# Split weights of the channel-major blocks: one fixed place in their tiles, or one of 16 places in turn

## The chip, the cores and the metric

The kernel runs on one core of a Trainium2 chip. The metric is the device time of one execution in microseconds (us), the median over several runs. The core has five engines with queues of their own: TensorE multiplies matrices, VectorE and ScalarE work element by element, GpSimd does small work and issues some transfers, and SyncE issues the weight transfers. On TensorE the loading of weights (the stationary operand) and the matmul that streams the other operand past them are recorded apart, as PEld and PE.

## The reference

One layer of a hybrid encoder for 256 tokens of width 2048, in float32. The normed input `n` is projected to queries, keys and values of a gated delta rule and of a dilated window attention; both are mixed by `w_out` and added to the residual stream. Then comes a gated MLP with a short convolution, and a last norm.

```
h = h + W_out [ GatedDeltaNet_bidir(n) ; DilatedWindowAttn(n) ],   n = RMSNorm(h)
up = conv3( RMSNorm(h) @ w_ffn_in )            # 2048 -> 2 x 5632
h = h + ( silu(gate) * val ) @ w_ffn_out       # 5632 -> 2048
out = RMSNorm(h)
```

The change touches the products with `w_in` (those for q, k, v and z of the delta rule and q and k of the attention) and with `w_ffn_in`.

## The kernel before

**Split products.** A float32 product is made of three matmuls on rounded parts: weights and activations are both split in a high part (the value as TensorE's fp32r type keeps it) and a low part (the rest). A product adds high x high, high x low and low x high. The activations lie split in `xcat`, for each of 16 tiles of 128 input channels 256 high and then 256 low columns, one for each token.

**Items.** A weight matrix comes in chunks of 1 MB over SyncE's queue into one of four tiles `raw`. A chunk is used in items of 1024 values for each partition. `split(u)` (line 257) has ScalarE copy an item's values into the high tile `his[u % 4]` (line 265) and VectorE subtract that from the raw values into the low tile `los[u % 4]` (line 266). The item's attribute `at` says at which float of these tiles, which are 1152 floats long, the 1024 values begin. `run_items` runs through all items in order: it keeps three items split ahead, issues an item's 24 matmuls (12 with 512 columns), and then gives other work (convolutions, attention, the delta rule's steps) a share of the engines' time; that work's own small matmuls and transposes come between the items on TensorE's queue.

**Channel-major blocks.** `cm_block` computes 128 output channels for all tokens. It has two items (input channels 0 to 1023 and 1024 to 2047), each with eight sets of 128 columns of weights. For each set the three lines 314, 315 and 316 load high, high and low weights, and stream the 256 high, 256 low and 256 high columns of `xcat`. All its items have `at = AT_CM = 32`. There are 80 such blocks in the input projection (24 for q, k and v of the delta rule, 8 for z, 48 for q and k of the attention) and 88 in the up projection, where all four tiles `his` and `los` are used in turn.

**Token-major items.** The values of the attention (`v_slab`, lines 382 to 384) take `xcat` as weights and stream the split weights in 256 columns, with `at = 0`. The output projection (`tm_group`, lines 1224 to 1226) loads the split mixed activations and streams split weights in 512 columns, with `at = AT_OUT = 72`; the last projection uses the same lines on `gth` and `gtl` with `at = 0`.

The order of the input projection is: 24 blocks, 8 blocks, then four times 12 blocks and three value slabs. In the up projection, the items of the first four blocks are interleaved, and after the transposes of the second norm (lines 1279 and 1298) no other work has matmuls until the end of that stage.

Of the kernel before, what the change touches and what calls it, by code (L numbers as in the profile page):

```python
# [24 lines left out]
NU = 4  # L25
LA = 3

AT_CM, AT_OUT = 32, 72
BV = 1300
BA = 1500  # L30
WAIT_FIRST = 8
# [54 lines left out]
def block_kernel(tc, A, out, dbg=None):  # L86
# [73 lines left out]
    done = set()  # L160
# [133 lines left out]
    def in_slab(w, c0, kh):  # L294
        return w[kh * 1024 : (kh + 1) * 1024, c0 : c0 + 256].rearrange("(k p) c -> p k c", p=P)

    accn = [0]

    def next_acc():
        accn[0] += 1  # L300
        return accs[accn[0] % len(accs)]

    def cm_block(ch, j, done, width=P):

        box = {}

        def half(kh):
            def mms(hi, lo):
                if kh == 0:
                    box["acc"] = next_acc()  # L310
                acc = box["acc"][:width, :T]
                for kk in range(8):
                    k = kh * 8 + kk
                    mm(acc, lhsT=hi[:, kk, :], rhs=xcat[:, k, :T], start=k == 0, stop=False)  # L314
                    mm(acc, lhsT=hi[:, kk, :], rhs=xcat[:, k, T:], start=False, stop=False)  # L315
                    mm(acc, lhsT=lo[:, kk, :], rhs=xcat[:, k, :T], start=False, stop=k == KT - 1)  # L316

            return mms

        for kh in range(2):  # L320
            Item(ch[kh], lambda t, j=j: t[:, :, j * width : (j + 1) * width], half(kh),
                 (lambda: done(box["acc"])) if kh else None, AT_CM)

    def evac(out_ap, acc, n=P, perm=None):

# [35 lines left out]
    def slab(w, c0, mk):  # L361
        ch = [Chunk(in_slab(w, c0, kh), (8, 256)) for kh in range(2)]
        for j in range(2):
            cm_block(ch, j, mk(j))
# [941 lines left out]
    for s in range(FT // 2):  # L1306
        if s == 0:
            ch = [Chunk(in_slab(w_up, w * FF, kh), (8, 256)) for kh in range(2) for w in range(2)]
            ch = [ch[0::2], ch[1::2]]
        else:  # L1310
            ch = [[Chunk(in_slab(w_up, w * FF + s * 256, kh), (8, 256)) for kh in range(2)] for w in range(2)]
        for w in range(2):
            for j in range(2):
                cm_block(ch[w], j, lambda acc, w=w, f=2 * s + j: hooks["up"](w, f, acc))
        if s == 0:
            items[-8:] = items[-8::2] + items[-7::2]
# [168 lines left out]
```

## Time and profile before

| | |
|---|---|
| median of 3 runs | 1546.69 us (1545.17 to 1550.15) |
| the profiled execution | 1545.1 us |
| its span, first to last instruction | 1543.3 us |
| TensorE busy | 1514.2 us, 11,531 matmuls |
| weight loads | 1443.4 us, 11,531 |
| VectorE busy | 1039.9 us |
| ScalarE busy | 827.9 us |
| GpSimd busy | 164.5 us |
| moved by the transfers | 301.20 MB, mean 195 GB/s |

A record of a matmul lasts longer than the distance to the next one's start, since matmuls overlap in the array. So a rate is read from starts in the timeline and from counts in a stretch, not from the length of a record. The stages in time are: input projection to about 700 us (the values of the attention in four portions from 292 us on), output projection to 797, up projection to 1295, last projection to 1536.

### The profile page before, as it was taken

What the parts mean: (1) busy time and instruction counts of PE and PEld (TensorE: products, weight loads), DVE (VectorE), ACT (ScalarE), POOL (GpSimd) and SP (SyncE); (2) the same over time, 40 slices, a digit from 0 to 9 for tenths busy, and PEclk for the clock granted to TensorE, in tenths of its full rate; (3) what the DMA queues carried; (4) which work ended last, traced back from release to release, by engine and by line L of the source; (5) the groups of instructions that cost most, each with busy time, mean ns of one, the idle gap of its engine ahead of it and who ended that gap; (6) DMA issues with size and microseconds to landing.
All of it is one profiled execution on the core that took longest, in us unless ns stands there. A gap on an engine that the chain in (4) does not pass through costs nothing.

```text
span 1543.3 us, 28173 instructions
## 1 busy us (share of the span) xinstructions
PE 1514.2 (98%) x11531; PEld 1443.4 (94%) x11531; DVE 1039.9 (67%) x1703; ACT 827.9 (54%) x1430; POOL 164.5 (11%) x245
## 2 busy tenths in 40 slices
PE   7999998999999999999999999999999999999997
PEld 7999998999999999997889999999999999888886
DVE  5878976979864666665557767677676676455454
ACT  5598874545555646554555544544544544344342
POOL 3264552000012202100000000000000000000000
PEclk9999999999999999999999999999999999999999
DMA  9656789646558636634765555565655657566552
GB/s 255 219 184 223 233 294 214 203 145 204 183 142 258 206 122 204 199 124 151 272 217 184 173 191 192 172 209 167 198 185 179 203 165 260 197 210 207 191 191 82
DMA packets 247283, 301.20 MB, mean 195 GB/s; under 512 B 10981, under 2 KB 207766, under 8 KB 246770
## 3 DMA queue, kind: packets, MB, share of 16 engines
q1 hardware_dynamic: 235602, 269.81, 54.4%
q0 software_dynamic: 11120, 29.01, 6.1%
q8 instruction: 90, 1.47, 0.4%
q10 hardware_dynamic: 432, 0.59, 0.1%
q14 instruction: 39, 0.32, 0.1%
HBM read 285.69 MB, written 13.65 MB: 194 GB/s over the span
## 4 chain that ended last, share of the span: by engine, by line
PE 91%; DMA 3%; ACT 2%; issue 2%; DVE 1%; POOL 1%; POOLq 0%; SPq 0%; ACTq 0%; DVEq 0%
PE bank L314 19%; PE bank L316 19%; PE bank L315 19%; PE bank L1224 7%; PE bank L1225 7%; PE bank L1226 7%; PE bank L382 3%; PE bank L383 3%; PE bank L384 3%; DMA raw<-in_w_in_dram 1%; PE bank L978 1%; PE bank L1024 1%; ACT hi L265 1%; PE bank L1019 1%; ACT kb L748 1%
## 5 line engine op out<-in xcount | busy, mean ns | idle before, releaser
L266 DVE TENSOR_TENSOR lo<-raw,hi 128x1024 fp32r<-128x1024 f32 x504 | 619.3, 1230 | 399.9 <-ACT hi L265 397.5
L265 ACT ACTIVATE hi<-raw 128x1024 fp32r<-128x1024 f32 x504 | 533.5, 1060 | 548.7 <-PE bank L315 262.5
L314 PE MATMUL bank<-xcat,hi 128*128 128x256 f32 x2688 | 758.4, 282 | 5.4 <-ACT qk L329 5.1
L315 PE MATMUL bank<-xcat,hi 128*128 128x256 f32 x2688 | 751.8, 280 | 0.0
L316 PE MATMUL bank<-xcat,lo 128*128 128x256 f32 x2688 | 751.6, 280 | 0.0
L314 PEld LDWEIGHTS bank<-xcat,hi 128*128 128x128 f32 x2688 | 506.2, 188 | 8.4 <-ACT qk L329 5.5
L315 PEld LDWEIGHTS bank<-xcat,hi 128*128 128x128 f32 x2688 | 512.0, 190 | 0.0
L316 PEld LDWEIGHTS bank<-xcat,lo 128*128 128x128 f32 x2688 | 505.6, 188 | 0.0
L1226 PE MATMUL bank<-hi,gtl 128*128 128x512 f32 x336 | 130.7, 389 | 0.0
L1225 PE MATMUL bank<-lo,gth 128*128 128x512 f32 x336 | 130.7, 389 | 0.0
L1224 PE MATMUL bank<-hi,gth 128*128 128x512 f32 x336 | 130.7, 389 | 0.0
L382 PE MATMUL bank<-hi,xcat 128*128 128x256 f32 x384 | 109.2, 284 | 0.0
L384 PE MATMUL bank<-hi,xcat 128*128 128x256 f32 x384 | 106.9, 278 | 0.0
L383 PE MATMUL bank<-lo,xcat 128*128 128x256 f32 x384 | 106.8, 278 | 0.0
L1224 PEld LDWEIGHTS bank<-hi,gth 128*128 128x128 f32 x336 | 63.1, 188 | 13.2
L1226 PEld LDWEIGHTS bank<-hi,gtl 128*128 128x128 f32 x336 | 63.1, 188 | 13.1
L1225 PEld LDWEIGHTS bank<-lo,gth 128*128 128x128 f32 x336 | 63.1, 188 | 13.0
L382 PEld LDWEIGHTS bank<-hi,xcat 128*128 128x128 f32 x384 | 72.4, 188 | 0.5
L384 PEld LDWEIGHTS bank<-hi,xcat 128*128 128x128 f32 x384 | 72.5, 189 | 0.0
L383 PEld LDWEIGHTS bank<-lo,xcat 128*128 128x128 f32 x384 | 72.3, 188 | 0.0
L1388 DVE SCALAR_TENSOR_TENSOR fy<-fpad,cwf,fy 128x256 f32<-128x256 f32 x132 | 63.4, 480 | 2.3
L1418 POOL DMA_DIRECT2D nfb<-in_norm_final_w_dram x1 | 0.6, 585 | 485.7 <-PE bank L316 485.7
(299 smaller groups left out, 1439.2 us busy)
## 6 DMA issues: line engine op xcount, KB each, us to landing
raw<-in_w_in_dram SPq DMA_DIRECT2D x104, 1024.0 KB, 5.7
raw<-in_w_ffn_in_dram SPq DMA_DIRECT2D x88, 1024.0 KB, 5.2
raw<-in_w_ffn_out_dram SPq DMA_DIRECT2D x44, 1024.0 KB, 5.0
raw<-in_w_out_dram SPq DMA_DIRECT2D x14, 1024.0 KB, 5.1
rec_d<-rec POOLq DMA_DIRECT2D x8, 768.0 KB, 7.1
rr<-rec_d POOLq DMA_DIRECT2D x6, 512.0 KB, 4.7
xt<-in_x_dram SPq DMA_DIRECT2D x4, 512.0 KB, 8.4
gam<-cg_d POOLq DMA_DIRECT2D x8, 256.0 KB, 8.7
```

The costliest lines, as they stand in the source:

```text
L265: ACT(hi, src, AF.Copy)
L266: V.tensor_sub(lo, src, hi.bitcast(F32))
L314: mm(acc, lhsT=hi[:, kk, :], rhs=xcat[:, k, :T], start=k == 0, stop=False)
L315: mm(acc, lhsT=hi[:, kk, :], rhs=xcat[:, k, T:], start=False, stop=False)
L316: mm(acc, lhsT=lo[:, kk, :], rhs=xcat[:, k, :T], start=False, stop=k == KT - 1)
L382: mm(o, lhsT=xh, rhs=hi[:, kk, :], start=k == 0 and t == 0, stop=False, skip_group_check=True)
L383: mm(o, lhsT=xh, rhs=lo[:, kk, :], start=False, stop=False, skip_group_check=True)
L384: mm(o, lhsT=xl, rhs=hi[:, kk, :], start=False, stop=k == KT - 1, skip_group_check=True)
L1224: mm(a[t], lhsT=xh, rhs=hi[:, kk, :], start=st, stop=False)
L1225: mm(a[t], lhsT=xh, rhs=lo[:, kk, :], start=False, stop=False)
L1226: mm(a[t], lhsT=xl, rhs=hi[:, kk, :], start=False, stop=sp_)
L1388: stt(y, pad[:, d : d + T], cwf[:, d, b : b + 1], y, op0=ALU.mult, op1=ALU.add)
```

## The change

`AT_CM` goes. `cm_block` counts its calls, and a block's two items begin at float `8 * (n % 16)` of their tiles, where n is the block's number, from 1 on: 8, 16, ... 120, 0, 8, and so on. A float has 4 bytes, so neighbouring blocks lie 32 bytes apart, modulo 512. The value slabs stay at 0, the output projection at 72, the last projection at 0.

```diff
-AT_CM, AT_OUT = 32, 72
+AT_OUT = 72
+AT_STEP, AT_N = 8, 16
...
-    accn = [0]
+    accn, blocks = [0], [0]
...
     def cm_block(ch, j, done, width=P):
 
         box = {}
+        blocks[0] += 1
+        at = AT_STEP * (blocks[0] % AT_N)
...
             Item(ch[kh], lambda t, j=j: t[:, :, j * width : (j + 1) * width], half(kh),
-                 (lambda: done(box["acc"])) if kh else None, AT_CM)
+                 (lambda: done(box["acc"])) if kh else None, at)
```

## Rows read from the trace of the kernel before

**Rows 1.** The page: busy time by engine; the chain that ended last, by line.
```profile
PE 1514.2 (98%) x11531; PEld 1443.4 (94%) x11531; DVE 1039.9 (67%) x1703; ACT 827.9 (54%) x1430; POOL 164.5 (11%) x245
...
PE bank L314 19%; PE bank L316 19%; PE bank L315 19%; PE bank L1224 7%; PE bank L1225 7%; PE bank L1226 7%; PE bank L382 3%; PE bank L383 3%; PE bank L384 3%; DMA raw<-in_w_in_dram 1%; PE bank L978 1%; PE bank L1024 1%; ACT hi L265 1%; PE bank L1019 1%; ACT kb L748 1%
```

**Rows 2.** Stretches: start:end, length, then PE, PEld, DVE, ACT, POOL; clock, DMA, GB/s.
```profile
25.00:293.00 268.00, 262.33 (x2270) 258.36 (x2269) 215.35 (x414) 193.35 (x443) 101.52 (x143) 0.99 0.76 230
293.00:700.00 407.00, 403.56 (x3433) 395.76 (x3432) 287.84 (x545) 226.10 (x435) 41.40 (x69) 1.00 0.57 179
...
812.00:1295.00 483.00, 483.00 (x4103) 483.00 (x4103) 342.20 (x514) 244.11 (x346) 0.00 (x0) 1.00 0.57 187
1295.00:1536.00 241.00, 239.75 (x1060) 198.22 (x1058) 119.32 (x116) 96.36 (x103) 4.37 (x6) 1.00 0.56 189
```

**Rows 3.** Timeline of TensorE's matmuls, input projection: start, length, line, operands.
```profile
370.13 0.28 PE L314 MATMUL bank<-xcat,hi 128*128 128x256 f32 x1
...
379.99 0.28 PE L314 MATMUL bank<-xcat,hi 128*128 128x256 f32 x1
```

**Rows 4.** Timeline of TensorE's matmuls, up projection.
```profile
1000.16 0.28 PE L314 MATMUL bank<-xcat,hi 128*128 128x256 f32 x1
...
1009.70 0.28 PE L314 MATMUL bank<-xcat,hi 128*128 128x256 f32 x1
```

**Rows 5.** Timeline of TensorE's matmuls, the last restart in the up projection.
```profile
811.39 0.60 PE L1298 MATMUL bank<-cst,ss 128*128 128x128 f32 x4
811.75 0.36 PE L314 MATMUL bank<-xcat,hi 128*128 128x256 f32 x1
...
812.19 0.28 PE L314 MATMUL bank<-xcat,hi 128*128 128x256 f32 x1
...
812.54 0.28 PE L314 MATMUL bank<-xcat,hi 128*128 128x256 f32 x1
```

**Rows 6.** Timeline of TensorE's matmuls, first and last item matmul of the input projection.
```profile
25.12 0.28 PE L314 MATMUL bank<-xcat,hi 128*128 128x256 f32 x1
...
698.04 0.28 PE L384 MATMUL bank<-hi,xcat 128*128 128x256 f32 x1
```

**Rows 7.** Timeline of TensorE's matmuls, passage from a channel-major block to values.
```profile
399.37 0.28 PE L314 MATMUL bank<-xcat,hi 128*128 128x256 f32 x1
...
399.71 0.28 PE L382 MATMUL bank<-hi,xcat 128*128 128x256 f32 x1
...
400.06 0.28 PE L382 MATMUL bank<-hi,xcat 128*128 128x256 f32 x1
...
400.41 0.28 PE L382 MATMUL bank<-hi,xcat 128*128 128x256 f32 x1
```

**Rows 8.** Timeline of TensorE's matmuls, an earlier passage of the same kind.
```profile
292.11 0.28 PE L314 MATMUL bank<-xcat,hi 128*128 128x256 f32 x1
...
292.46 0.29 PE L382 MATMUL bank<-hi,xcat 128*128 128x256 f32 x1
...
292.82 0.28 PE L382 MATMUL bank<-hi,xcat 128*128 128x256 f32 x1
...
293.16 0.28 PE L382 MATMUL bank<-hi,xcat 128*128 128x256 f32 x1
```

**Rows 9.** Groups by line and form on VectorE, 797 to 1295 and 1295 to 1524 us.
```profile
L266 DVE TENSOR_TENSOR lo<-raw,hi 128x1024 fp32r<-128x1024 f32 x176 | 215.7, 1225 | 142.4 <-ACT hi L265 141.5
...
L266 DVE TENSOR_TENSOR lo<-raw,hi 128x1024 fp32r<-128x1024 f32 x84 | 102.5, 1225 | 112.7 <-ACT hi L265 112.7
```

**Rows 10.** Timeline of TensorE's matmuls, output projection and last projection.
```profile
717.11 0.39 PE L1224 MATMUL bank<-hi,mxh 128*128 128x512 f32 x1
...
717.79 0.39 PE L1224 MATMUL bank<-hi,mxh 128*128 128x512 f32 x1
...
1399.95 0.39 PE L1224 MATMUL bank<-hi,gth 128*128 128x512 f32 x1
...
1400.63 0.39 PE L1224 MATMUL bank<-hi,gth 128*128 128x512 f32 x1
```

## The prediction, made before the changed kernel ran

> **What bounds the kernel now.** I read the page first. TensorE is busy for 98% of the span, and of the chain of work that ended last 19% each lies on lines 314, 315 and 316, the three matmuls of a channel-major product [rows 1]. The stretches by stage say the same more sharply: from 812 to 1295 us, the up projection, TensorE is busy for 483.00 of 483.00 us while VectorE works for 342 and ScalarE for 244, and the last projection, 1295 to 1536, is nearly as full [rows 2]. So nothing feeds TensorE too late there; the time is the number of matmuls times the step from one start to the next.
>
> That step has two values. Between 370.13 and 379.99 us lie 87 steps in 9.86 us, 113.33 ns each [rows 3]; between 1000.16 and 1009.70 lie 81 steps in 9.54 us, 117.78 ns each [rows 4]. Both stretches run the same lines on operands of one shape, from the same tiles, with the split weights at the same place in them (32), at a granted clock of 1.00, the 2.4 GHz level [rows 2]. I call them the short and the long step; the difference is 117.78 - 113.33 = 4.45 ns a matmul.
>
> Which one runs is decided at a restart and then stays. After the four small matmuls of line 1298, line 314 restarts at 811.75 us; its next start, at 812.19, contains the restart, and from there three steps take 0.35 us (3 x 117.8 = 353 ns; three short ones would take 340) [rows 5]. It stays long through 4,103 matmuls, the count of the stretch [rows 2], over all four tiles, eight weight positions in each, and four accumulators. From the first to the last channel-major or value matmul of the input projection (first and last row in [rows 6], 4,992 starts between and with them) I count the 4,991 steps between neighbours: 3,091 short, 1,656 long, and 244 others, which are restarts, the first few matmuls after one, and some 3 us of doubled steps near 270 us. Of 103 uninterrupted runs there, 63 settle on the short step and 40 on the long one, and none changes later of itself.
>
> One event changes it without an interruption: the passage between the channel-major products, whose weights lie at 32 in the split tiles, and the value products (lines 382 to 384), which stream the split tiles from 0 and take their weights from xcat. At 399.71 us the short step becomes long (three steps take 0.34 us before it, 0.35 and 0.35 after) [rows 7], at 292.46 long becomes short (0.35 before, 0.36 in the passage, 0.34 after) [rows 8], and at 329.68, 437.44 and 520.31 the same view shows short to long twice and long to short once. Five passages, five flips. At such a passage the placement changes, but so do the roles of the tiles.
>
> **The change part by part.** It removes and adds no instruction, no DMA and no wait, and moves nothing in any queue. It moves where the 168 channel-major blocks (80 of the input projection, 88 of the up projection) keep their split weights: block n starts at 8 x (n mod 16) floats instead of 32. Reads and writes of one item move together.
>
> Splitting itself: VectorE writes the low part of an item in 1225 ns with the weights at 32, and in 1225 ns in the last projection with them at 0 [rows 9]. I take nothing, and half of the last digit (0.5 ns) an item either way; TensorE's work hides it in the up projection, where VectorE is idle for 141 of 483 us [rows 2]. Without that cover, 336 items would give 0.2 us.
>
> The matmuls: the moved weights are the operand that TensorE loads. The output projection streams its split weights from 72, the last projection from 0, with 512 columns, and both step by 0.68 us for three, 226.7 ns [rows 10]. So 288 and 0 bytes do not differ for a streamed operand; a loaded one at another place is nowhere in the trace by itself. Its cost is bounded by the two steps: if every block boundary could set the step anew, the up projection gains at most 4,103 x 4.45 = 18.3 us (all short) and at least nothing (all long, as now); a longer step at this clock is in no row, and I take none. In the input projection only what lies behind a block boundary inside an uninterrupted run can change: 1,296 matmuls on the short step (+5.8 us if all turn long) and 240 on the long one (-1.1 us).
>
> I take the passages of [rows 7, 8] as the nearest rows: a jump in the placement between two matmuls that follow each other is what flips the step, and from now on there is one at every block boundary. If each boundary flips it, half of the up projection runs short: -9.1 us; in the input projection somewhat over half of the 1,296 turn long and of the 240 short, +3.3 - 0.6 = +2.7. Together -6.4. If instead a boundary acts as a restart, 63 of 103 come up short: -11.2 in the up projection, 0.39 x 5.8 - 0.61 x 1.1 = +1.6 before, together -9.6. The middle is -8.0 us. The output and last projections and the 48 value items keep their places; the values' restarts may fall otherwise, which I leave in the range.
>
> The profiled execution took 1545.1 us (span 1543.3 and 1.8 around it), 1.6 below the median of 1546.69. 1545.1 - 8.0 = 1537.1, and 1538.7 at the median's level. Its own range is 1533 to 1543.
>
> **The rivals.**
>
> *The place plays no part*: 1546.7. For it: the step stays at one value while loads go over four tiles and eight positions in each [rows 2, 4], both steps occur at place 32 [rows 3, 4], and 72 and 0 do not differ when streamed [rows 10]. The flips at the passages could come from the exchange of roles alone. Against it: those positions differ by whole 128-column blocks, and a shift inside one block appears only at the passages. The Trainium skill, SBUF — State Buffer, section "A bandwidth-pool intuition that's wrong (but worth ruling out)", gives TensorE's weight load a read port of its own beside the streaming operand's. By that rule where the loaded weights lie could not disturb the stream, and the sum would be 0; no row here tests it, and the two steps at one and the same place agree with it so far.
>
> *Short everywhere*: a boundary releases the long step and nothing brings it back. -18.3 - 1.1 = -19.4, 1527.3. For it: after a restart the short step is the commoner one, 63 of 103 [rows 6], and two passages led to it; against: three of five passages went from short to long.
>
> *Slower*: a boundary breaks the short step and leaves the long one. Its place is the input projection, whose uninterrupted short runs of more than a block hold the 1,296 matmuls; the up projection has nothing to lose, since it runs long already. +5.8, 1552.5; with all 3,091 short steps of the input projection made long it would be +13.8, 1560.4. It decides from the point where the long step outlasts the boundaries of the up projection. For it: the three passages from short to long, and 4,103 matmuls without a way out; against: two passages out of the long step.
>
> **How the numbers follow.** Forecast 0.40, no part 0.29, short everywhere 0.14, slower 0.17. Below 0.3% (4.6 us, about what can be told from no change here), so between 1542.1 and 1551.3, lie the second case, a small part of the forecast (0.05) and of the last (0.03). Faster 0.35 + 0.14 = 0.49; same 0.05 + 0.29 + 0.03 = 0.37; slower 0.14. The range from 1525 to 1554 holds all but the far end of the last case (1560.4) and an up projection all short whose input projection's restarts turn short as well.
>
> **What would show it.** In the changed kernel's view of TensorE from about 812 to 1290 us, steps of 0.113 and 0.118 must alternate in stretches of 48 matmuls or multiples, with the change at a first matmul of line 314 of a block; the up projection must then last about 474 us in place of 483. One step throughout with 483 us says that the place plays no part; 465 us that short wins; a longer input projection (25 to 700 us) with an unchanged up projection is the slower case. A step above 0.118 in some blocks, or VectorE's splits off 1225 ns, would make the prediction wrong in a way I have no row for.

## The result, and the profile after

The changed kernel took 1556.67 us (median of 4 runs, 1555.06 to 1556.94), the kernel before 1548.42 beside it (4 runs): a ratio of 1.0061, 95% interval [1.0046, 1.0076]. It is slower, by 0.6%. The forecast was 1538.7, and the range ended at 1554.

The page of the changed kernel, in the two rows that answer to [rows 1] (lines below 300 have moved down by 1, those from 314 on by 3):

```profile
PE 1529.1 (98%) x11531; PEld 1458.8 (94%) x11531; DVE 1041.2 (67%) x1703; ACT 828.4 (53%) x1430; POOL 162.4 (10%) x245
...
PE bank L317 19%; PE bank L319 19%; PE bank L318 19%; PE bank L1227 7%; PE bank L1228 7%; PE bank L1229 7%; PE bank L385 3%; PE bank L387 3%; PE bank L386 3%; DMA raw<-in_w_in_dram 1%; PE bank L981 1%; PE bank L1027 1%; PE bank L1022 1%; ACT kb L751 1%; DMA rec_d<-rec 1%
```

TensorE is still the bound, with the same number of matmuls, and takes longer for them. The stretches that answer to [rows 2], with the same columns, and one more, from 830 to 1270 us, which lies inside the up projection in every kernel below:

```profile
25.00:293.00 268.00, 263.27 (x2228) 259.56 (x2227) 211.71 (x409) 191.25 (x441) 99.49 (x143) 0.99 0.74 224
293.00:700.00 407.00, 407.00 (x3428) 399.74 (x3426) 286.31 (x529) 223.51 (x422) 40.64 (x67) 1.00 0.58 180
812.00:1295.00 483.00, 483.00 (x4084) 483.00 (x4083) 340.27 (x519) 242.06 (x343) 0.71 (x1) 1.00 0.57 185
1295.00:1536.00 241.00, 241.00 (x1111) 201.59 (x1111) 121.92 (x118) 101.22 (x110) 3.43 (x5) 1.00 0.58 197
...
830.00:1270.00 440.00, 440.00 (x3718) 440.00 (x3717) 310.76 (x469) 220.76 (x314) 0.00 (x0) 1.00 0.57 187
```

From 830 to 1270 us TensorE is busy throughout at a granted clock of 1.00, so the length by the count is the step: 440 / 3718 = 118.34 ns. The same stretch of the kernel before reads:

```profile
830.00:1270.00 440.00, 440.00 (x3739) 440.00 (x3738) 311.57 (x469) 219.95 (x314) 0.00 (x0) 1.00 0.57 187
```

That is 117.68 ns. This one row measures the step of the up projection in every kernel below.

The timeline shows what the steps depend on. In the changed kernel, TensorE's first channel-major matmul and the last value matmul of the input projection (they answer to [rows 6]), and the ends of four stretches without a pause (a pause is other work's matmuls, or a wait, between two item matmuls; the first matmul behind it is a restart):

```profile
26.01 0.28 PE L317 MATMUL bank<-xcat,hi 128*128 128x256 f32 x1
...
70.63 0.28 PE L317 MATMUL bank<-xcat,hi 128*128 128x256 f32 x1
...
73.35 0.28 PE L317 MATMUL bank<-xcat,hi 128*128 128x256 f32 x1
...
706.37 0.28 PE L387 MATMUL bank<-hi,xcat 128*128 128x256 f32 x1
...
937.20 0.28 PE L317 MATMUL bank<-xcat,hi 128*128 128x256 f32 x1
...
942.85 0.28 PE L317 MATMUL bank<-xcat,hi 128*128 128x256 f32 x1
...
951.38 0.28 PE L317 MATMUL bank<-xcat,hi 128*128 128x256 f32 x1
...
954.26 0.28 PE L317 MATMUL bank<-xcat,hi 128*128 128x256 f32 x1
...
965.59 0.28 PE L317 MATMUL bank<-xcat,hi 128*128 128x256 f32 x1
...
971.22 0.28 PE L317 MATMUL bank<-xcat,hi 128*128 128x256 f32 x1
```

From 70.63 the first item of a block at place 64 runs: 24 steps in 2.72 us, 113.3 ns, the short step. From 937.20 another block at 64: 48 steps in 5.65 us, 117.7, the long one. From 951.38 the second item of a block at 80: 24 steps in 2.88 us, 120.0 ns, a steady step that the kernel before has nowhere. From 965.59 a block at 104: 48 steps in 5.63 us, 117.3, mixed of steps from 113 to 120. By the timeline's starts, the mean step of the up projection's blocks 85 to 168 at each place is the same for places 64 apart to 0.01 ns:

| place (floats), and that + 64 | 0 | 8 | 16 | 24 | 32 | 40 | 48 | 56 |
|---|---|---|---|---|---|---|---|---|
| mean step, ns | 117.73 | 117.97 | 119.78 | 118.25 | 117.86 | 117.36 | 118.51 | 119.77 |

Steady runs of 113.3 ns occur in blocks at 0, 32, 64 and 96 alone. Between the profiled executions (1545.1 and 1556.45, +11.35) the time went as follows. The input projection, from first start to last, takes 706.37 - 26.01 = 680.4 us in place of 672.9 [rows 6]: +7.4. The channel-major steps that I count there below 131 ns (3,742, before 3,738) have a mean of 118.03 ns in place of 114.88 (578 are below 115.5 ns, and so counted as short, in place of 2,481): +11.8; the values gain 0.8 and the pauses are 3.5 us shorter. The up projection, to the first matmul of the last one, takes 501.3 in place of 498.4 us: +2.9, of 4,224 steps at 118.37 in place of 117.67. The first item starts 0.9 us later, which no place explains.

### The profile page after: what moved, and what is told of

The parts are those of the page before. It is cut to its first block, busy times and chain, and to the rows that moved or that the text cites. A ratio compares the mean times of both kernels' runs of the same rounds, so it can differ in the third digit from the quotient of the medians.

```text
span 1554.7 us, 28173 instructions
## 1 busy us (share of the span) xinstructions
PE 1529.1 (98%) x11531; PEld 1458.8 (94%) x11531; DVE 1041.2 (67%) x1703; ACT 828.4 (53%) x1430; POOL 162.4 (10%) x245
## 4 chain that ended last, share of the span: by engine, by line
PE 91%; DMA 3%; ACT 2%; issue 2%; DVE 1%; POOL 1%; POOLq 0%; SPq 0%; ACTq 0%; DVEq 0%
PE bank L317 19%; PE bank L319 19%; PE bank L318 19%; PE bank L1227 7%; PE bank L1228 7%; PE bank L1229 7%; PE bank L385 3%; PE bank L387 3%; PE bank L386 3%; DMA raw<-in_w_in_dram 1%; PE bank L981 1%; PE bank L1027 1%; PE bank L1022 1%; ACT kb L751 1%; DMA rec_d<-rec 1%
```

## The experiments

Each kernel was timed in 3 rounds beside the kernel before (medians of it 1545.58 to 1547.23 in the four sessions). The first four set two theories beside the prediction's rule: that the *place* itself decides which step is possible, or that the *jump* between blocks throws the stream to the long step. After each quoted expectation stands the row of 830 to 1270 us with [rows 2]'s columns.

**One fixed place, 16.**

```diff
-AT_CM, AT_OUT = 32, 72
+AT_CM, AT_OUT = 16, 72
```

> The kernel before with one change: all channel-major weights begin at float 16, without any jump between blocks. Theory P (the place itself decides: only places that are multiples of 32 floats allow the short step of 113.3 ns, and a block at 16 steps at 119 to 120 ns wherever it stands): no short step in any channel-major block; 2,481 steps of the projection grow by about 6.5 ns (+16 us), 1,256 by 2 ns (+2.5), the 4,113 of the up projection by 2.1 ns (+8.6); about 1575 us, 1570 to 1580. Theory J (the jump from one place to another throws the step to the long one; any place that stays is as good as 32): runs settle on 113.3 or 117.8 as before, 1540 to 1553 us.

Measured: 1566.55 us (1565.87 to 1569.55), ratio 1.0138 [1.0113, 1.0164].

```profile
830.00:1270.00 440.00, 440.00 (x3669) 440.00 (x3668) 307.12 (x462) 218.11 (x310) 0.00 (x0) 1.00 0.56 182
```

440 / 3669 = 119.9 ns. The timeline shows the steady step, 81 steps between these two starts, as many as in [rows 4]:

```profile
1000.28 0.28 PE L314 MATMUL bank<-xcat,hi 128*128 128x256 f32 x1
...
1010.00 0.28 PE L314 MATMUL bank<-xcat,hi 128*128 128x256 f32 x1
```

9.72 / 81 = 120.0 ns. No block jumps here, yet it is slower than the changed kernel: the jump theory falls. Of the input projection's channel-major steps 4 are short and 3,757 are not.

**Jumps between multiples of 32 alone** (places 0, 32, 64, 96).

```diff
-AT_STEP, AT_N = 8, 16
+AT_STEP, AT_N = 32, 4
```

> The changed kernel with four places in turn, 0, 32, 64 and 96 floats, so the place still jumps at every block boundary. P: multiples of 32 allow the short step, so runs on it go on across boundaries; 1,500 to 3,000 short steps among the channel-major matmuls of the projection (before 2,481, changed kernel 578), 1528 to 1553 us by how restarts fall. J: every boundary breaks the short step; under 900 short steps there, and 1553 to 1560 us as with 16 places. The prediction's own rule (a boundary flips or redraws the step) would leave both steps mixed in the up projection, 9 us under the kernel before.

Measured: 1532.05 us (1530.21 to 1534.08), ratio 0.9909 [0.9888, 0.993], faster than both kernels.

```profile
830.00:1270.00 440.00, 440.00 (x3884) 440.00 (x3884) 323.11 (x489) 229.21 (x326) 0.00 (x0) 1.00 0.60 194
```

440 / 3884 = 113.3 ns, the short step through every jump. The input projection's channel-major blocks count 2,055 short steps and 1,667 long ones, and it ends 4.5 us later than before; the up projection is 18 us shorter.

**Places in turn in the up projection alone**, 32 in the input projection.

```diff
-        at = AT_STEP * (blocks[0] % AT_N)
+        at = AT_STEP * (blocks[0] % AT_N) if blocks[0] > 80 else 32
```

> The places in turn in the 88 blocks of the up projection alone; the 80 of the input projection stay at 32. P: the up projection steps at 118.4 in the mean in place of 117.7, +2.9 us, and the input projection is as before: 1548 to 1553 us. J: the same within 1 us, since the up projection is long already. The prediction's rule: -6 to -11 us, 1536 to 1542.

Measured: 1549.9 us (1546.03 to 1551.56), ratio 1.0016 [1.0003, 1.0029].

```profile
830.00:1270.00 440.00, 440.00 (x3718) 440.00 (x3717) 310.14 (x467) 218.94 (x310) 0.00 (x0) 1.00 0.57 185
```

The count is the changed kernel's to the matmul: the up projection costs what it cost there, and the rest of the loss, 1.0061 against 1.0016, is the input projection's. The prediction's rule asked for 1536 to 1542 here.

**One fixed place, 40.**

```diff
-AT_CM, AT_OUT = 32, 72
+AT_CM, AT_OUT = 40, 72
```

> The kernel before with all channel-major weights at float 40, the place whose blocks had the lowest step in the up projection of the changed kernel (117.36 ns). P: no short step in the projection (+10 us for its 2,481), up projection -0.4 ns a matmul (-1.6): about 1555 us, 1552 to 1563 (in the projection this place also showed 118.6 to 120). J: 1540 to 1553 us with short steps present.

Measured: 1555.67 us (1555.22 to 1557.02), ratio 1.0063 [1.0043, 1.0083].

```profile
830.00:1270.00 440.00, 440.00 (x3752) 440.00 (x3752) 313.33 (x471) 222.62 (x315) 0.00 (x0) 1.00 0.58 187
```

117.3 ns: a pattern of five steps between 115 and 120 ns, over and over. In the up projection that is below the long step (117.8); the time is lost in the input projection. There a steady short step never comes, and the restarts choose between patterns here too: of its 160 items, 88 have a mean near 117.4 ns, 68 near 118.7 and 3 near 120.1.

The next four ask what in the place counts, and what sets the step where both are possible.

**Weights and streamed operand moved together**: place 16, and the streamed tile 16 floats (64 bytes) lower.

```diff
-    xcat = xp.tile([P, KT, 512], F32R, name="xcat")
+    xcat_t = xp.tile([P, KT * 512 + 16], F32R, name="xcat")
+    xcat = xcat_t[:, : KT * 512].rearrange("p (k c) -> p k c", k=KT)
...
-                 (lambda: done(box["acc"])) if u == 3 else None)
+                 (lambda: done(box["acc"])) if u == 3 else None, AT_V)
```

with AT_CM = 16 and AT_V = 112.

> The weights of the channel-major blocks at float 16, as in the run with fixed place 16, but the streamed tile (xcat) moved by 16 floats too, so that the distance between the two is that of the kernel before; the value blocks' weights stand at float 112, which keeps theirs. If the distance between the loaded weights and the streamed columns decides which step is possible: 113.3 ns steps come back in the input projection (some 1,000 to 2,700 of its channel-major steps), the up projection steps at 113.3 or 117.8 throughout, 1530 to 1553 us. If the place in the tile decides by itself: no step of 113.3 in any channel-major block, 120.0 ns there, the values slower as well (float 112 is no multiple of 32), 1563 to 1574 us.

Measured: 1547.03 us (1544.58 to 1547.7), ratio 0.9999 [0.9989, 1.0009].

```profile
830.00:1270.00 440.00, 440.00 (x3738) 440.00 (x3738) 312.27 (x470) 220.03 (x312) 0.00 (x0) 1.00 0.57 187
```

117.7 ns, as before, and the short step is back in the input projection; 216 steps lie between these starts of its timeline:

```profile
226.25 0.28 PE L315 MATMUL bank<-xcat,hi 128*128 128x256 f32 x1
...
250.73 0.28 PE L315 MATMUL bank<-xcat,hi 128*128 128x256 f32 x1
```

24.48 / 216 = 113.3 ns. The same place 16 that gave 1566.55 costs nothing here. So what counts is where the loaded weights and the streamed columns lie against each other, the distance of their addresses, and not the place in the tile. One such pair was tried.

**One fixed place, 64.**

```diff
-AT_CM, AT_OUT = 32, 72
+AT_CM, AT_OUT = 64, 72
```

> One fixed place, 64: a multiple of 32 like the kernel before, and without the jumps of the version with step 32. If the multiple of 32 only allows the short step and each restart of the stream draws: both steps occur, as before; the up projection, which has few restarts, is at 113.3 or 117.8 for long stretches; 1525 to 1553 us by the draw. If the jumps between multiples of 32 are what brought the short step to the up projection in the version with step 32: long there as before, 117.8, and 1545 to 1550 us. If 32 itself is special: no short step in the channel-major blocks, 1553 us or more.

Measured: 1553.09 us (1552.06 to 1553.91), ratio 1.0039 [1.0025, 1.0052].

```profile
830.00:1270.00 440.00, 440.00 (x3738) 440.00 (x3738) 313.12 (x471) 221.31 (x314) 0.00 (x0) 1.00 0.57 187
```

The up projection is that of before to one matmul. Short and long are again the steady steps, but the draw differs: of 69 pauses in the input projection behind which a channel-major item goes on, 68 lead to the long step and 1 to the short one; at place 32 in the kernel before, 45 of 71 led to the short one. The time is just over my interval's upper end, since I had taken the draw to be the same at all multiples of 32. That the up projection stays long without jumps fits the second case as well, which so far is not excluded.

**One fixed place, 36.**

```diff
-AT_CM, AT_OUT = 32, 72
+AT_CM, AT_OUT = 36, 72
```

> One fixed place, 36, four floats past that of before. If any departure from a multiple of 32 floats takes the short step away: no run of 113.3 ns steps in the channel-major blocks, a mean of 117 to 120 ns, 1551 to 1567 us. If the rule goes by coarser grains (eight floats or more), 36 is like 32: both steps as before, 1530 to 1553 us.

Measured: 1561.28 us (1560.14 to 1561.71), ratio 1.0094 [1.0075, 1.0113].

```profile
830.00:1270.00 440.00, 440.00 (x3706) 440.00 (x3705) 310.35 (x467) 219.86 (x312) 0.00 (x0) 1.00 0.57 186
```

118.7 ns, and no steady run of the short step in either projection: four floats (16 bytes) are enough to lose it.

**Six restarts in the up projection** of the kernel before: one transpose, its result unused, ahead of blocks 92, 104, 116, 128, 140 and 152.

```diff
+                    if again:
+                        bk = SB.get()
+                        nc.tensor.transpose(bk[:, :P], ident, ident)
+                        SB.put(bk)
```

> The kernel before with one 128-column transpose (its result is unused) ahead of each of six channel-major blocks of the up projection, 12 blocks apart. If a restart of the stream draws the step anew: in the up projection, steady 117.8 ns before, some of the six stretches of 24 items (576 steps) go over to 113.3 ns, 2.6 us less for each; six restarts cost at most some 0.3 us each; 1532 to 1549 us, with the change of step at the transposes. If the stage keeps the step that it entered with, whatever interrupts it: 117.8 throughout, 1547 to 1549 us.

Measured: 1540.61 us (1536.05 to 1541.47), ratio 0.9956 [0.9937, 0.9974].

```profile
830.00:1270.00 440.00, 440.00 (x3803) 440.00 (x3802) 315.79 (x476) 224.10 (x318) 0.00 (x0) 1.00 0.59 189
```

The timeline around the second of them (L315; a start's distance to the third before it is three steps):

```profile
927.87 0.28 PE L320 MATMUL bank<-xcat,hi 128*128 128x256 f32 x1
...
928.22 0.28 PE L320 MATMUL bank<-xcat,hi 128*128 128x256 f32 x1
928.34 0.28 PE L321 MATMUL bank<-xcat,hi 128*128 128x256 f32 x1
928.46 0.28 PE L322 MATMUL bank<-xcat,lo 128*128 128x256 f32 x1
928.57 0.27 PE L315 MATMUL bank<-cst 128*128 128x128 f32 x1
928.60 0.36 PE L320 MATMUL bank<-xcat,hi 128*128 128x256 f32 x1
928.80 0.28 PE L321 MATMUL bank<-xcat,hi 128*128 128x256 f32 x1
928.92 0.29 PE L322 MATMUL bank<-xcat,lo 128*128 128x256 f32 x1
929.04 0.28 PE L320 MATMUL bank<-xcat,hi 128*128 128x256 f32 x1
929.16 0.28 PE L321 MATMUL bank<-xcat,hi 128*128 128x256 f32 x1
929.27 0.28 PE L322 MATMUL bank<-xcat,lo 128*128 128x256 f32 x1
929.39 0.28 PE L320 MATMUL bank<-xcat,hi 128*128 128x256 f32 x1
```

Before it three steps take 0.35 us; from 929.16 on, behind the first steps after the pause, they are short, 0.23 us for the two to 929.39, and the block's next 20 keep 113.3 ns. The six stretches came out long, short, short, long, short, long, each change of step at a transpose and none in between: a pause draws the step, which then holds.

The next three ask whether step 32 owes its short up projection to a lucky draw or to its jumps.

**Step 32 in the up projection alone.**

```diff
-        at = AT_STEP * (blocks[0] % AT_N)
+        at = AT_STEP * (blocks[0] % AT_N) if blocks[0] > 80 else 32
```

(with AT_STEP, AT_N = 32, 4)

> Step 32 (0, 32, 64, 96) in the up projection alone; the input projection at 32 as in the kernel before. The input projection should end as before, about 698 us into the span. In the up projection both steps are possible by my theory and the restarts at its beginning draw: at 113.3 as with step 32 throughout, 1527 to 1531 us; at 117.7, 1545 to 1550 us; anything in between only with a restart between. If jumping between multiples of 32 is itself what gives the short step: 1527 to 1531 us only.

Measured: 1528.5 us (1526.47 to 1531.91), ratio 0.9891 [0.9868, 0.9913].

```profile
830.00:1270.00 440.00, 440.00 (x3885) 440.00 (x3884) 321.77 (x486) 228.88 (x324) 0.00 (x0) 1.00 0.60 194
```

The input projection ends at 698.1 us as before, and the up projection is short. The time alone agrees with a lucky draw as well as with the jumps. The trace tells them apart. These starts lie behind the last restart of the stage's beginning, at 811.79 us, in the second items of blocks 82 (place 64) and 83 (place 96), which follow each other there (the last row is the first start of block 84's):

```profile
812.22 0.28 PE L317 MATMUL bank<-xcat,hi 128*128 128x256 f32 x1
...
814.34 0.28 PE L317 MATMUL bank<-xcat,hi 128*128 128x256 f32 x1
...
815.39 0.28 PE L317 MATMUL bank<-xcat,hi 128*128 128x256 f32 x1
...
817.43 0.28 PE L317 MATMUL bank<-xcat,hi 128*128 128x256 f32 x1
```

Up to 814.34, 18 steps take 2.12 us (117.8 ns): the restart fell to the long step. At 814.69 block 83 begins without a pause, and from 815.39 on 18 steps take 2.04 us (113.3), which lasts to the end of the stage. So the jump from 64 to 96 brought the short step here; in the run with step 32 throughout the same happens at 820.28.

**One of the six restarts alone**, ahead of block 104 of the kernel before.

```diff
-        again = blocks[0] in (92, 104, 116, 128, 140, 152)
+        again = blocks[0] == 104
```

> The kernel before with one of the six transposes, the one ahead of block 104, after which the short step came in the run with six. All that runs ahead of it in the stage is the same but for one earlier transpose. If a restart draws and the stage then holds: 117.8 ns up to block 104 and then 113.3 to the end of the up projection if the draw falls as it did, about 3,100 steps by 4.45 ns or 14 us less, 1531 to 1536 us; 117.8 throughout and 1546 to 1549 us if it falls the other way. If the short step in the run with six came from something else at that time (not the transpose's being there): a change of step at some other place.

Measured: 1547.27 us (1543.97 to 1549.81), ratio 1.001 [0.9997, 1.0023].

```profile
830.00:1270.00 440.00, 440.00 (x3738) 440.00 (x3737) 311.56 (x469) 220.10 (x313) 0.00 (x0) 1.00 0.58 187
```

The same transpose, which led to the short step behind one more like it, leads to the long one here, 117.7 ns to the end. So which way a restart falls can't be read from the transpose itself. Nor do the times look like a new draw at every execution: all ten lie between 1543.97 and 1549.81 us, where the short step to the end would give 14 us less, and no execution of the kernel before, in any session, lies 18 us below the others. For one compiled kernel such a restart seems to fall the same way each time; why is open.

**Six restarts and step 32 together.**

```diff
         at = AT_STEP * (blocks[0] % AT_N)
+        again = blocks[0] in (92, 104, 116, 128, 140, 152)
```

> Step 32 in all channel-major blocks, with the six transposes in the up projection. If restarts draw, and the jumps between multiples of 32 leave the step as it is: some of the six stretches go to 117.8 ns (2.6 us each for 24 items) and the change stands at the transposes, 1532 to 1546 us. If the jumps between multiples of 32 hold the stream at the short step: 113.3 throughout but for the step or two at each transpose, 1531 to 1534 us.

Measured: 1536.03 us (1532.74 to 1538.53), ratio 0.9937 [0.9916, 0.9959].

```profile
830.00:1270.00 440.00, 440.00 (x3854) 440.00 (x3854) 319.86 (x483) 227.05 (x321) 0.00 (x0) 1.00 0.60 193
```

Each of the six restarts falls to the long step, and each stretch becomes short again without a pause: the first after one block, at the jump from 0 to 32, the other five after three blocks, at the jump from 64 to 96. The timeline behind the first: starts of the second item of block 92 (place 0), and of both items of block 93 (place 32):

```profile
865.30 0.28 PE L322 MATMUL bank<-xcat,hi 128*128 128x256 f32 x1
...
868.13 0.28 PE L322 MATMUL bank<-xcat,hi 128*128 128x256 f32 x1
...
870.85 0.28 PE L322 MATMUL bank<-xcat,hi 128*128 128x256 f32 x1
```

24 steps take 2.83 us (117.9 ns), then, with nothing between them but the jump from 0 to 32, 2.72 (113.3). Both of the written theories were half right: the restarts draw, and the jumps don't hold the stream at the short step but bring it back. Counted from the timeline, in this run and the two with step 32 before it: of 42 jumps without a pause from an even to an odd multiple (0 to 32, 64 to 96) that met the long step, 25 ended it; of 17 the other way none did; of 283 that met the short step, none broke it.

**The jumps inside the item.** All channel-major weights in rows of 160, 128, 160, 128, ... floats, so that each item goes from an even to an odd multiple twice.

```diff
+        if it.at is None:
+            src = src.rearrange("p (a e) c -> p a e c", e=2)
+            hi, lo = [aview(t[u % NU][:, :], 0, [(288, 4), (160, 2), (1, P)]) for t in (his, los)]
...
-                    mm(acc, lhsT=hi[:, kk, :], rhs=xcat[:, k, :T], start=k == 0, stop=False)
+                    mm(acc, lhsT=hi[:, kk // 2, kk % 2, :], rhs=xcat[:, k, :T], start=k == 0, stop=False)
```

> The jumps of 32 floats put inside the blocks: every channel-major item's eight weight slices lie at 0, 160, 288, 448, 576, 736, 864 and 1024 in its tile, so that the place changes from an even to an odd multiple of 32 after the first and the fifth slice, and back after the third and the seventh. In the traces with step 32, a long step has gone over to the short one at 25 of 42 uninterrupted jumps from an even to an odd multiple, never at 17 jumps the other way, and a short step has outlived every jump. If this holds for jumps inside an item: a stream that restarts long is short again within an item or two, long steps in the input projection's channel-major blocks fall from about 1,000 to 500-900, the up projection is short throughout, 1522 to 1530 us. If such jumps work between blocks only (new bank, new sum): the items look like those at the fixed place 64, mostly 117.8, 1548 to 1556 us. If the two conversions slow down by their broken rows, the stream waits for weights: pauses before items, over 1530 us with short steps.

Measured: 1526.2 us (1523.67 to 1527.95), ratio 0.9864 [0.9847, 0.9881].

```profile
830.00:1270.00 440.00, 440.00 (x3885) 440.00 (x3884) 322.49 (x487) 229.33 (x326) 0.00 (x0) 1.00 0.60 193
```

One item behind a pause in the input projection, the first matmuls of its slices 2, 5, 6, 7 and 8 and of the next item:

```profile
34.49 0.28 PE L318 MATMUL bank<-xcat,hi 128*128 128x256 f32 x1
...
35.55 0.28 PE L318 MATMUL bank<-xcat,hi 128*128 128x256 f32 x1
...
35.91 0.28 PE L318 MATMUL bank<-xcat,hi 128*128 128x256 f32 x1
...
36.25 0.28 PE L318 MATMUL bank<-xcat,hi 128*128 128x256 f32 x1
...
36.59 0.28 PE L318 MATMUL bank<-xcat,hi 128*128 128x256 f32 x1
...
36.93 0.28 PE L318 MATMUL bank<-xcat,hi 128*128 128x256 f32 x1
```

From 34.49 nine steps take 1.06 us (117.8); the step turns at 35.91, slice 6, the second jump from even to odd, and from there three take 0.34. The long steps of the input projection's channel-major blocks fall to 245 of 3,719 (1,257 of 3,738 before), fewer than I expected. This version beats both kernels; that it beats the 1528.5 above is not shown, since the two intervals of the ratio overlap.

## Why the prediction was wrong

*What bounds the kernel* held: TensorE's step decides, the splits are still off the path, and VectorE's still take 1225 ns in the up and the last projection, as [rows 9] let expect.

*The step that failed* is the one that begins "I take the passages of [rows 7, 8] as the nearest rows: a jump in the placement between two matmuls that follow each other is what flips the step". It made the jump the cause and left the new place itself without a price. The runs show that the place comes first. The distance between the loaded and the streamed address, to 16 bytes, decides which steps are possible (fixed 16, 36 and 40, and 16 with both operands moved); at 12 of the 16 places of the change no steady short step was seen. At the other four, the stream enters from a place 8 floats before and lands long: 30 of 34 uninterrupted entries in the changed kernel, against the half or 63 of 103 that I took. So the up projection got none of the 9.1 to 11.2 us, and the input projection lost more than +2.7.

*The bound that failed* is "a longer step at this clock is in no row, and I take none". 120.0 ns at 16 and 80, and about as much at 56 and 120 in the second item of a block, is such a step. "Bounded by the two steps" let two values seen at one place stand for a place that no row had; the up projection's +2.9 us lies outside that bound, on the side that I had set to nothing. One count in that sum was low besides: 382 long steps of the input projection lie behind a block boundary without a pause, not 240 (the run that ends in the passage at 292.46 us holds 144 of them), so -1.1 us should have been -1.7. That moves the forecast by less than 0.5 us.

*The comparison that misled* in the case against any effect was 72 and 0 for streamed operands [rows 10]: it is of 512 columns, and of weights streamed, and says nothing of weights loaded against 256 streamed columns.

*What stood.* Two levels, chosen at a restart and then kept, are confirmed by the six transposes; at the fixed places 32 and 64 neither step turns into the other without a pause. The slower rival had the place of the loss right, the input projection's short runs, +7.4 us beside its +5.8 to +13.8, and the prediction's last paragraph named a step above 0.118 as what would make the prediction wrong. That rival's mechanism, a boundary that breaks the short step, is not what happens: boundaries between multiples of 32 leave it alone 283 times of 283, and it is the place behind a boundary that ends it. The rival's up projection, with nothing to lose, was wrong too. What *short everywhere* asked of the up projection, 18.3 us less, came with jumps of 32 floats in place of 8: 18.0 us.

The Trainium skill, SBUF — State Buffer, section "A bandwidth-pool intuition that's wrong (but worth ruling out)", gives the weight load a read port of its own, from which I concluded that its place could not disturb the stream. These runs disagree with that conclusion: with nothing but that place changed (fixed 16), the step goes from 113.3 or 117.8 ns to 120.0. Whether the load has a port of its own they do not show.

*What stays open.* No run shows what in the memory the distance stands for, why a jump from even to odd ends the long step and the reverse does not, why pauses at place 32 lead to the short step more often than not (45 of 71) and at 64 almost never (1 of 69), or what makes one restart fall long and another short. Whether the flips at [rows 7, 8] come from the new distance at a passage or from the roles was not tried. Nor were other places for the value blocks tried, half of whose steps are still long in the last version (606 of 1,125).

## What to carry to other kernels

Where TensorE is full and its starts are a steady few per cent apart between stretches of the same instruction, vary the distance between the addresses of the loaded and the streamed operand: here a shift of 16 bytes in one tile moved this kernel by 0.9%, and the right layout by 1.4% the other way, with no instruction changed in number. A level that a trace shows at one address is no bound for another address; measure a place fixed before a place in turn. And where a pause leads to one of two steps, don't count on the better one: arrange something that leads back to the good one, as the jumps inside the item do.

## What the runs showed of the hardware that I had not expected

For a 128x128 load with 256 streamed FP32 columns at a granted clock of 1.00: steady steps of 113.3, 117.8 and 120.0 ns and mixed patterns between, depending on where the weights lie against the streamed columns, and alike to 0.01 ns in the mean for places 64 floats apart (the changed kernel's up projection). A single 128-column transpose between two matmuls costs about 0.1 us (928.46 to 928.80 in the run with six, 0.34 us for what takes 0.23 otherwise) and can set the step anew for all that follows without a pause, 576 matmuls between two of the six: six of them were worth 6 us, one alone nothing.
